# Probing only the even rows of a sorted segment mean, and fetching the odd rows' boundaries from their neighbours

## The chip, the cores and the metric

The kernel runs on one core of a Trainium2 chip. The time is the device time of one execution in microseconds (us). A run's time is about 2 us longer than the span of the instructions in its profile. A run is marked slow when it lies more than 1.5% above the fastest of the same kernel; ratios use fast runs alone.

Engines: DVE is VectorE, ACT is ScalarE, POOL is GpSimd, SP is SyncE, whose queue issues the large loads. PE (TensorE) does next to nothing here.

## The reference

```python
def setup_inputs():
    n = 10_000_000
    num_segments = 10000
    return {
        "data": np.random.randn(n).astype(np.float32),
        "segment_ids": np.sort(np.random.randint(0, num_segments, n)),
    }

def reference(data, segment_ids):
    num_segments = int(segment_ids.max()) + 1
    sums = np.zeros(num_segments, dtype=np.float32)
    counts = np.zeros(num_segments, dtype=np.float32)
    np.add.at(sums, segment_ids, data)
    np.add.at(counts, segment_ids, 1)
    return sums / np.maximum(counts, 1)
```

The ids are sorted and 64 bits wide, and a segment has about 1,000 elements. So one need not read all 80 MB of ids: it is enough to find where each segment ends.

## The kernel before

Each of 128 partitions holds 78,125 consecutive elements, cut into 90 rows of `L = 875` (the last one shorter). A row is shorter than nearly every segment, so it contains at most one boundary, or the kernel takes a slow general path. For every row the kernel works in five steps:

1. *Probe*: 5 single ids per row, one every `S = 175`, loaded by the SP queue as 8-byte pieces (15 loads of 6 rows each).
2. *Look* (DVE, six small instructions for a group of 6 rows): from the probes, find the block of 175 ids in which the id changes.
3. *Fetch* (POOL): an indirect DMA brings that block, 175 ids from each partition, into a ring of 18 windows.
4. *Window sum* (ACT) and *cut* (DVE): the sum of the window's ids gives the exact boundary `KK`.
5. *Split* (DVE, the large one): the row's data left of the boundary is summed. ACT sums the whole row (*total*); right is total minus left.

The distance in rows between asking for a window and needing it is written into the program: the look, with its fetches, of the group that begins at row g runs after the split of row g−9 (`X_LOOK = 9`), and its cut after the split of row g−1. That is 8 rows between ask and use.

```python
GROUPS = [6] * 15
X_PROBE, X_DATA, X_LOOK, RING, HALVES = 11, 26, 9, 18, 66
# ... cut: constants, general path ...
    dpool = ctx.enter_context(tc.tile_pool(name="dpool", bufs=18))      # 18 tiles of two rows
# ...
    def load_probes(g):
        a = 0 if g == 0 else K * bounds[g] + 1
        b = min(K * bounds[g + 1] + 1, NPR)
        nc.sync.dma_start(out=pr_flat[:, a:b], in_=ids_p[:, a * S : (b - 1) * S + 1 : S])
# ... cut: first_look, steps s1 to s5; s5 makes IDX, the block's address, and ends with ...
            gather(g)

    def gather(g):
        for r in range(bounds[g], bounds[g + 1]):
            nc.gpsimd.indirect_dma_start(
                out=GT[:, r % RING, :], out_offset=None, in_=ids2d[:],
                in_offset=bass.IndirectOffsetOnAxis(ap=IDX[:, r : r + 1], axis=0),
                bounds_check=N - W, oob_is_err=False,
            )

    def add_ids(r):
        nc.scalar.activation(
            out=junk_a[:, 0:W], in_=gt32[:, r % RING, 0 : 2 * W : 2], func=ACT.Copy,
            accum_out=GS[:, r : r + 1],
        )

    def second_look(a, b):                                              # the cut
        def s1():
            nc.vector.scalar_tensor_tensor(
                out=KK[:, a:b], in0=YY[:, a:b], scalar=float(S // K), in1=GS[:, a:b],
                op0=ALU.mult, op1=ALU.subtract,
            )
# ...
    def total(r):
        nc.scalar.activation(out=junk_a[:, 0:n], in_=d, func=ACT.Copy, accum_out=t)

    def split(r):
        nc.vector.scalar_tensor_tensor(
            out=junk_v[:, 0:n], in0=iota[:, 0:n], scalar=KK[:, r : r + 1], in1=d,
            op0=ALU.is_lt, op1=ALU.mult, accum_out=A[:, r : r + 1],
        )
# ... cut: combining partitions, output; then the schedule ...
    for a, b in zip(bounds[1:], bounds[2:]):
        if a < HALVES:
            put(a - 1, second_look(a, b))
# ...
    for g in range(HEAD, NG):
        if g < NG - 1:
            put(max(bounds[g] - X_LOOK, 0), first_look(g), 5)
# ... per row r: add_ids up to row r + 6, then
            total(r)
            split(r)
            for f in after[r]:
                f()
```

Of the kernel before, what the change touches and what calls it, by code (L numbers as in the profile page):

```python
# [9 lines left out]
FP32 = mybir.dt.float32  # L10
BF16 = mybir.dt.bfloat16
I32 = mybir.dt.int32
# [5 lines left out]
P = 128  # L18
D = 78125
# [10 lines left out]
GROUPS = [6] * 15  # L30
X_PROBE = 11
X_DATA = 26
X_LOOK = 9
RING = 18
HALVES = 66
# [82 lines left out]
def kernel(  # L118
# [9 lines left out]
    assert N == P * D and NSEG == 10000 and sum(GROUPS) == NR  # L128
# [14 lines left out]
    def x_sum(r):  # L143
        return 6 if r < HALVES else 5


    pr = cpool.tile([P, NR + 1, K], I64, name="pr")
    pr_flat = pr.rearrange("p r k -> p (r k)")
    pr32 = pr.bitcast(I32)
    snt = cpool.tile([P, 1], I64, name="snt")  # L150
    snt32 = snt.bitcast(I32)
    NPR = (D + S - 1) // S
    assert NPR == (NR - 1) * K + 2

    bounds = [0]
    for g in GROUPS:
        bounds.append(bounds[-1] + g)

    def load_probes(g):
        a = 0 if g == 0 else K * bounds[g] + 1  # L160
        b = min(K * bounds[g + 1] + 1, NPR)
        nc.sync.dma_start(out=pr_flat[:, a:b], in_=ids_p[:, a * S : (b - 1) * S + 1 : S])
# [17 lines left out]
    GT = gpool.tile([P, RING, W], I64, name="GT")  # L180
    gt32 = GT.bitcast(I32)

    def view(ap, dims):
# [3 lines left out]
        out=gt32[:, :, 0 : 2 * W : 2], in_=view(q5[:, 0, 0:1], [[0, RING], [0, W]]), func=ACT.Copy  # L187
    )

    wb_i = cpool.tile([P, NR], I32, name="wb_i")  # L190
    wb = cpool.tile([P, NR], FP32, name="wb")
    nc.gpsimd.iota(wb_i[:, 0 : NR - 1], pattern=[[L, NR - 1]], base=-S, channel_multiplier=D)
    nc.gpsimd.iota(wb_i[:, NR - 1 : NR], pattern=[[0, 1]], base=(NR - 1) * L - TAIL, channel_multiplier=D)
    nc.vector.tensor_copy(out=wb, in_=wb_i)
    i_i = cpool.tile([P, L], I32, name="i_i")
# [42 lines left out]
    VI = pr32[:, :, 0]  # L238
    SG = cpool.tile([P, NR], FP32, name="SG")
    ST = cpool.tile([P, NR], FP32, name="ST")  # L240
    YY = cpool.tile([P, NR], FP32, name="YY")
    IDX = cpool.tile([P, NR], I32, name="IDX")
    GS = cpool.tile([P, NR], FP32, name="GS")
# [12 lines left out]
    def first_look(g):  # L256

        a, b = bounds[g], bounds[g + 1]
        n = b - a
        far = fpool.tile([P, n], FP32, name="far", bufs=3)  # L260
        last = b == NR
        v = nc.vector

        def s1():
            if last:
                m = NR * K + 1 - NPR
                v.tensor_copy(
                    out=pr_flat.bitcast(I32)[:, 2 * NPR : 2 * (NPR + m)].rearrange("p (a b) -> p a b", b=2),
                    in_=view(snt32[:, 0:1], [[0, m], [1, 2]]),
                )  # L270
            v.tensor_reduce(out=SG[:, a:b], in_=pr32[:, a:b, 0 : 2 * K : 2], axis=AX.X, op=ALU.add)  # L271

        def s2():
            v.scalar_tensor_tensor(  # L274
                out=ST[:, a:b], in0=VI[:, a + 1 : b + 1], scalar=float(K), in1=SG[:, a:b],
                op0=ALU.mult, op1=ALU.subtract,
            )

        def s3():
            v.tensor_scalar(out=far, in0=ST[:, a:b], scalar1=0.0, scalar2=FAR, op0=ALU.is_equal, op1=ALU.mult)  # L280

        def s4():
            v.tensor_add(out=ST[:, a:b], in0=ST[:, a:b], in1=far)  # L283

        def s5():
            for c, d, w in [(a, b - 1, S), (b - 1, b, TAIL)] if last else [(a, b, S)]:
                v.scalar_tensor_tensor(  # L287
                    out=IDX[:, c:d], in0=ST[:, c:d], scalar=float(w), in1=wb[:, c:d], op0=ALU.mult, op1=ALU.add
                )
            v.scalar_tensor_tensor(  # L290
                out=YY[:, a:b], in0=ST[:, a:b], scalar=float(K + 1), in1=SG[:, a:b], op0=ALU.mult, op1=ALU.add
            )
            if last:
                v.tensor_scalar(
                    out=tl, in0=ST[:, NR - 1 : NR], scalar1=-1.0, scalar2=float(TAIL - S),
                    op0=ALU.add, op1=ALU.mult,
                )
            gather(g)

        return [s1, s2, s3, s4, s5]  # L300

    def gather(g):
        for r in range(bounds[g], bounds[g + 1]):
            nc.gpsimd.indirect_dma_start(  # L304
                out=GT[:, r % RING, :],
                out_offset=None,
                in_=ids2d[:],
                in_offset=bass.IndirectOffsetOnAxis(ap=IDX[:, r : r + 1], axis=0),
                bounds_check=N - W,
                oob_is_err=False,  # L310
            )

    def add_ids(r):
        nc.scalar.activation(  # L314
            out=junk_a[:, 0:W], in_=gt32[:, r % RING, 0 : 2 * W : 2], func=ACT.Copy,
            accum_out=GS[:, r : r + 1],
        )

    def second_look(a, b):
        def s1():  # L320
            nc.vector.scalar_tensor_tensor(  # L321
                out=KK[:, a:b], in0=YY[:, a:b], scalar=float(S // K), in1=GS[:, a:b],
                op0=ALU.mult, op1=ALU.subtract,
            )
            if b == NR:
                nc.vector.tensor_add(out=KK[:, NR - 1 : NR], in0=KK[:, NR - 1 : NR], in1=tl)

        return [s1]
# [54 lines left out]
    bad = cpool.tile([P, 2 * NX + 8], FP32, name="bad")  # L383
# [14 lines left out]
    def edges(a, b):  # L398
        nc.vector.tensor_sub(out=BT[:, a:b], in0=VI[:, a + 1 : b + 1], in1=VI[:, a:b])
# [6 lines left out]
    def extend():  # L406

        def s1():
            nc.vector.tensor_sub(out=B[:, 0:E], in0=T[:, 0:E], in1=A[:, 0:E])
            nc.vector.tensor_copy(out=V[:, 0 : E + 1], in_=VI[:, 0 : E + 1])  # L410
            edges(0, E)
# [41 lines left out]
    def keys(a, b):  # L453
        def s1():
            if a == 0:
                nc.vector.tensor_add(out=base1, in0=VI[:, 0:1], in1=pin)

        def s2():
            v = VI[:, a:b] if b <= NR else V[:, a:b]
            nc.vector.tensor_scalar(  # L460
                out=KEY[:, PAD + a : PAD + b], in0=v, scalar1=base1[:, 0:1], scalar2=None, op0=ALU.subtract
            )
            if b <= NR:
                edges(a, b)
            if a == 0:
                nc.vector.tensor_sub(out=delta, in0=sp, in1=base1)
# [55 lines left out]
    def check_columns():  # L522
# [3 lines left out]
                out=bad[:, NC + i : NC + i + 1], in0=sp, scalar=float(c), in1=VI[:, r : r + 1],  # L526
                op0=ALU.add, op1=o,
            )
            for i, c, r, o in ((5, C1, R1, ALU.is_gt), (6, C2, RM, ALU.is_gt), (7, CA, RM - 1, ALU.is_le))
        ]  # L530
# [151 lines left out]
    def pick(e, o, c0, n, a, b):  # L682
# [3 lines left out]
        def s1():  # L686
            c = min(b, NR)
            e.tensor_scalar(
                out=KL[:, a - R1 : c - R1], in0=VI[:, a:c], scalar1=sp[:, 0:1], scalar2=None, op0=ALU.subtract
# [77 lines left out]
    NG = len(GROUPS)  # L767
# [3 lines left out]
    HEAD = 3  # L771

# [7 lines left out]
    for g in range(HEAD):  # L780
        after[-1] += first_look(g)
    after[-1] += second_look(0, GROUPS[0])
    for a, b in zip(bounds[1:], bounds[2:]):
        if a < HALVES:
            put(a - 1, second_look(a, b))
        else:
            put(a - 1, second_look(a, a + 3))
            put(a + 2, second_look(a + 3, b))
    for g in range(HEAD, NG):
        if g < NG - 1:  # L790
            put(max(bounds[g] - X_LOOK, 0), first_look(g), 5)
# [28 lines left out]
    look = bounds[NG - 1] - X_LOOK - 2  # L820
# [6 lines left out]
    put(look, first_look(NG - 1), 99)  # L827
    put(look + 2, counts(R1, RM), 2)
    put(look, pick(nc.gpsimd, pb[:, :, RE - RM :], C2, NO - C2, RE, R2), 99)
    put(look + 1, edges_of(RE, NR))  # L830
    put(look + 4, single(0, NX, bad[:, NX:NC]) + verdict())
    put(look + 4, [
        lambda: v.tensor_scalar(out=nbl, in0=BT[:, NR - 2 : NR], scalar1=-1.0, scalar2=None, op0=ALU.mult)
    ])
    after[look + 7].append(lambda: verdict_reg.append(nc.values_load(badi[0:1, 0:1], min_val=0, max_val=1)))
# [11 lines left out]
    pnext = 0  # L847
    nt = 0
    gs = 0
    for r in range(-X_PROBE - X_DATA, NR):  # L850
        while pnext < NG and bounds[pnext] <= r + X_PROBE + pnext // (NG - 1) + X_DATA:
            load_probes(pnext)
            pnext += 1
            if pnext == 1:
                load_data(0)
                nt = 1
        while nt < NT and 2 * nt <= r + X_DATA:
            load_data(nt)
            nt += 1
# [5 lines left out]
        if r == -1:  # L865
            for f in after[r][: 5 * HEAD]:
                f()
        while r >= -1 and gs < NR and gs <= r + x_sum(gs):
            add_ids(gs)
            gs += 1  # L870
        if r == -1:
            for f in after[r][5 * HEAD :]:
                f()
        if r >= 0:
            total(r)
            split(r)
            for f in after[r]:
                f()
# [31 lines left out]
```

## Time and profile before

| | before |
|---|---|
| time, median of 3 (lowest to highest) | 189.97 us (189.69 to 190.56) |
| packets under 512 bytes | 60,016 |
| DMA share by stretch of time, from the windows view: 0–23, 23–60, 60–100, 100–140, 140–175, 175–190 us | 0.97, 1.07, 1.03, 1.03, 1.06, 0.12 |
| DVE busy / ACT busy / POOL busy | 140.9 / 136.5 / 99.8 us |
| last data packet ends | 177.4 us |
| row 24 / row 88 split begins | 63.4 / 183.8 us |

The profiled execution is marked slow (192.2 us).

The first lines are from the page of the kernel before: the busy tenths of DVE and DMA in 40 slices, the packets, and the share of 16 engines' time that each queue's packets took (q1 loads data and probes, q0 the fetches).

```profile
DVE  6521295969478792956978999566899969999991
...
DMA  6999999999999999999999999999999999999100
...
DMA packets 70163, 54.61 MB, mean 287 GB/s; under 512 B 60016, under 2 KB 60584, under 8 KB 70151
...
q1 hardware_dynamic: 64219, 40.50, 73.0%
q0 software_dynamic: 5760, 14.01, 23.2%
```

DMA is at nine tenths or more in 36 of 40 slices, DVE is not, and the traffic ends with the work.

The costliest groups on the same page: busy us, mean ns of one, then the idle time just before these instructions and what ended most of it.

```profile
L304 POOL DMA_INDIRECT GT<-in_segment_ids_dram,IDX x90 | 90.9, 1010 | 70.1 <-ACT junk_a L314 28.1
L339 DVE SCALAR_TENSOR_TENSOR junk_v<-iota,q,data_t 128x875 bf16<-128x875 f32 x90 | 100.4, 1116 | 7.4 <-DMA data_t<-in_data_dram 6.0
...
L314 ACT ACTIVATE junk_a<-GT 128x175 bf16<-128x175 int32 x90 | 32.4, 361 | 41.9 <-DMA GT<-in_segment_ids_dram,IDX 37.0
L321 DVE SCALAR_TENSOR_TENSOR q<-YY,GS 128x6 f32<-128x6 f32 (+1 forms) x19 | 3.2, 171 | 27.1 <-ACT junk_a L314 18.2
```

L304 is the fetch, L339 the split, L314 the window sum, L321 the cut. The waits view of the same kernel (us in total, times, longest):

```profile
ACT junk_a L314 <- DMA GT<-in_segment_ids_dram,IDX: 37.0, 22, 8.6
...
DVE q L321 <- ACT junk_a L314: 18.2, 8, 3.6
DVE q L321 <- issue: 7.6, 1, 7.6
DVE junk_v L339 <- DMA data_t<-in_data_dram: 6.0, 6, 1.9
```

How long a fetch takes is seen in the chain of waits (start us, us, what):

```profile
12.42 1.00 POOL GT L304
...
15.03 6.80 DMA GT<-in_segment_ids_dram,IDX
...
59.67 7.07 DMA GT<-in_segment_ids_dram,IDX
...
143.78 7.02 DMA GT<-in_segment_ids_dram,IDX
...
155.22 19.10 DMA data_t<-in_data_dram
```

A fetch takes about 7 us here from the start of its POOL record to landing, while that record lasts 1.0 us. The chain is made of fetches and of data by turns; the last long piece is 19.1 us of data. This agrees with the Trainium skill (Perfetto Trace Analysis, "DMA Instruction — SWDGE (GPSIMD)"), which says that the profiler's end of such an instruction is the end of descriptor generation and not of the data's movement.

### The profile page before, as it was taken

The page shows a single profiled execution, that of the slowest core. Times are in us where ns is not written, and L with a number is a line of the kernel's source. Part 1 is how long each engine was busy: PE and PEld are TensorE (multiplying, and loading weights), DVE is VectorE, ACT ScalarE, POOL GpSimd, SP SyncE. Part 2 cuts the span into 40 slices and gives each one's busy share as a digit, 9 for nine tenths or more (in the row PEclk, how much of TensorE's full clock was granted, in tenths as well). Part 3 has the DMA queues.
Part 4 walks back from the last instruction along what each step waited for, and adds up shares of the span by engine and source line. Part 5 has one row for each costly group of instructions (what it writes and reads, how often), then busy time and mean ns, then how long its engine had stood idle before and what let it go on. Part 6 is the DMA issues. An engine that isn't in the chain of part 4 may idle for free.

```text
span 190.2 us, 1434 instructions
## 1 busy us (share of the span) xinstructions
PE 1.6 (1%) x6; PEld 1.4 (1%) x6; DVE 140.9 (74%) x438; ACT 136.5 (72%) x362; POOL 99.8 (52%) x119
## 2 busy tenths in 40 slices
PE   0000000000002000000000000000000000010000
PEld 0000000000001000000000000000000000010000
DVE  6521295969478792956978999566899969999991
ACT  8011498995989499698685948959868594999930
POOL 5577875065753737266272572726638278782000
DMA  6999999999999999999999999999999999999100
GB/s 29 174 188 414 271 330 413 174 405 261 331 412 176 401 284 297 412 147 374 311 284 408 138 370 339 266 392 186 401 301 274 299 349 412 397 405 399 54 0 8
DMA packets 70163, 54.61 MB, mean 287 GB/s; under 512 B 60016, under 2 KB 60584, under 8 KB 70151
## 3 DMA queue, kind: packets, MB, share of 16 engines
q1 hardware_dynamic: 64219, 40.50, 73.0%
q0 software_dynamic: 5760, 14.01, 23.2%
q14 instruction: 12, 0.10, 0.2%
q10 hardware_dynamic: 172, 0.00, 0.1%
HBM read 56.59 MB, written 0.04 MB: 298 GB/s over the span
## 4 chain that ended last, share of the span: by engine, by line
DMA 45%; issue 27%; ACT 9%; POOL 8%; DVE 7%; POOLq 0%; ACTq 0%; DVEq 0%
DMA GT<-in_segment_ids_dram,IDX 23%; DMA data_t<-in_data_dram 22%; POOL GT L304 7%; ACT junk_a L334 5%; ACT junk_a L314 4%; DVE junk_v L339 2%; DVE jj L235 1%; POOL i_i L197 0%; POOLq L304 0%; DVE most L744 0%; DVE add L736 0%; DVE PS L561 0%; DVE add L744 0%; DVE ps L558 0%; DVE most L750 0%
## 5 line engine op out<-in xcount | busy, mean ns | idle before, releaser
L304 POOL DMA_INDIRECT GT<-in_segment_ids_dram,IDX x90 | 90.9, 1010 | 70.1 <-ACT junk_a L314 28.1
L339 DVE SCALAR_TENSOR_TENSOR junk_v<-iota,q,data_t 128x875 bf16<-128x875 f32 x90 | 100.4, 1116 | 7.4 <-DMA data_t<-in_data_dram 6.0
L334 ACT ACTIVATE junk_a<-data_t 128x875 bf16<-128x875 f32 x90 | 83.6, 929 | 3.5 <-ACT junk_a L314 0.7
L314 ACT ACTIVATE junk_a<-GT 128x175 bf16<-128x175 int32 x90 | 32.4, 361 | 41.9 <-DMA GT<-in_segment_ids_dram,IDX 37.0
L321 DVE SCALAR_TENSOR_TENSOR q<-YY,GS 128x6 f32<-128x6 f32 (+1 forms) x19 | 3.2, 171 | 27.1 <-ACT junk_a L314 18.2
L314 ACT ACTIVATION_READ_ACCUMULATOR junk_a<-GT 128x1 f32 x90 | 16.8, 186 | 0.0
L334 ACT ACTIVATION_READ_ACCUMULATOR junk_a<-data_t 128x1 f32 x90 | 16.8, 186 | 0.0
L339 DVE DVE_READ_ACCUMULATOR junk_v<-iota,q,data_t 128x1 f32 x90 | 7.4, 82 | 0.0
L271 DVE TENSOR_REDUCE SG<-pr 128x6 f32<-128x30 int32 x15 | 2.7, 180 | 5.4 <-DMA pr<-in_segment_ids_dram 5.3
L186 ACT ACTIVATE GT<-q 128x3150 int32<-128x3150 f32 x1 | 3.0, 2998 | 0.0
L280 DVE TENSOR_SCALAR far<-ST 128x6 f32<-128x6 f32 x15 | 2.6, 171 | 0.5
L287 DVE SCALAR_TENSOR_TENSOR IDX<-ST,wb 128x6 int32<-128x6 f32 (+2 forms) x16 | 2.6, 165 | 0.5
L274 DVE SCALAR_TENSOR_TENSOR ST<-pr,SG 128x6 f32<-128x6 int32 x15 | 2.5, 165 | 0.5
L283 DVE TENSOR_TENSOR ST<-ST,far 128x6 f32<-128x6 f32 x15 | 2.5, 165 | 0.5
L290 DVE SCALAR_TENSOR_TENSOR YY<-ST,SG 128x6 f32<-128x6 f32 x15 | 2.4, 158 | 0.0
L235 DVE CAST jj<-jj_i 128x128 f32<-128x128 int32 x1 | 1.5, 1484 | 0.7 <-POOL jj_i L234 0.7
L186 ACT ACT_TABLE_LOAD x1 | 1.3, 1283 | 0.7 <-PEq L894 0.7
L703 POOL TENSOR_SCALAR pb<-pb 128x168 f32<-128x168 f32 (+1 forms) x2 | 1.6, 784 | 0.2
L589 DVE TENSOR_TENSOR_SCAN FFP<-NBP,FFP,XX 128x16 f32<-128x16 f32 (+2 forms) x4 | 1.5, 382 | 0.0
L543 PE MATMUL badp<-bads,ones 128*128 128x1 f32 x2 | 0.6, 362 | 106.3 <-DVE bads L542 106.3
L583 DVE TENSOR_TENSOR q<-T,q 128x44 f32<-128x44 f32 (+3 forms) x4 | 0.7, 180 | 0.9 <-DVE RB L574 0.4
L736 POOL TENSOR_TENSOR xa<-pa,RG 128x528 f32<-128x528 f32 x1 | 1.2, 1247 | 0.2 <-DVE RG L733 0.2
(129 smaller groups left out, 44.3 us busy)
## 6 DMA issues: line engine op xcount, KB each, us to landing
data_t<-in_data_dram SPq DMA_DIRECT2D x44, 875.0 KB
GT<-in_segment_ids_dram,IDX POOLq DMA_INDIRECT x90
data_t<-in_data_dram SPq DMA_DIRECT2D x1, 437.5 KB
pr<-in_segment_ids_dram SPq DMA_DIRECT2D x13, 30.0 KB
data_t<-in_data_dram SPq DMA_DIRECT2D x1, 125.0 KB
out_dram<-OUT SPq DMA_DIRECT2D x1, 36.6 KB
pr<-in_segment_ids_dram SPq DMA_DIRECT2D x1, 31.0 KB
pr<-in_segment_ids_dram SPq DMA_DIRECT2D x1, 26.0 KB
```

The lines of the kernel that those rows point to most:

```text
L186: nc.scalar.activation(out=gt32[:, :, 0 : 2 * W : 2], in_=view(q5[:, 0, 0:1], [[0, RING], [0, W]]), func=ACT.Copy)
L235: nc.vector.tensor_copy(out=jj, in_=jj_i)
L271: v.tensor_reduce(out=SG[:, a:b], in_=pr32[:, a:b, 0 : 2 * K : 2], axis=AX.X, op=ALU.add)
L274: v.scalar_tensor_tensor(out=ST[:, a:b], in0=VI[:, a + 1 : b + 1], scalar=float(K), in1=SG[:, a:b], op0=ALU.mult, op1=ALU.subtract,)
L280: v.tensor_scalar(out=far, in0=ST[:, a:b], scalar1=0.0, scalar2=FAR, op0=ALU.is_equal, op1=ALU.mult)
L283: v.tensor_add(out=ST[:, a:b], in0=ST[:, a:b], in1=far)
L287: v.scalar_tensor_tensor(out=IDX[:, c:d], in0=ST[:, c:d], scalar=float(w), in1=wb[:, c:d], op0=ALU.mult, op1=ALU.add)
L304: nc.gpsimd.indirect_dma_start(out=GT[:, r % RING, :], out_offset=None, in_=ids2d[:], in_offset=bass.IndirectOffsetOnAxis(ap=IDX[:, r : r ...
L314: nc.scalar.activation(out=junk_a[:, 0:W], in_=gt32[:, r % RING, 0 : 2 * W : 2], func=ACT.Copy, accum_out=GS[:, r : r + 1],)
L321: nc.vector.scalar_tensor_tensor(out=KK[:, a:b], in0=YY[:, a:b], scalar=float(S // K), in1=GS[:, a:b], op0=ALU.mult, op1=ALU.subtract,)
L334: nc.scalar.activation(out=junk_a[:, 0:n], in_=d, func=ACT.Copy, accum_out=t)
L339: nc.vector.scalar_tensor_tensor(out=junk_v[:, 0:n], in0=iota[:, 0:n], scalar=KK[:, r : r + 1], in1=d, op0=ALU.is_lt, op1=ALU.mult, accum_ ...
```

## The change

The intent is to save DMA time. Neighbouring boundaries lie about one segment apart, so an odd row's boundary must lie near the middle between the boundaries of the even rows around it. So only even rows are probed (6 points each, so that the row's last id is known too). An odd row's 208 ids are fetched around the mean of its neighbours' exact boundaries. A check at the end finds any boundary that lay outside its 208 ids and then takes the general path. The last 7 rows are all probed, and the row totals on ACT run up to 6 rows ahead in the first part.

```diff
-GROUPS = [6] * 15
+EVEN = [3, 3, 3, 3, 6, 6, 6, 6, 6]          # groups of even rows
+WO = 208
+    def load_pairs(a, b):                    # 42 loads of one even row each
+        nc.sync.dma_start(
+            out=pr[:, a:b, :],
+            in_=bass.AP(ids_p.tensor, ids_p.offset + 2 * L * a, [list(ids_p.ap[0]), [2 * L, b - a], [S, K + 1]]),
+        )
# ... cut: gather and add_ids now take both kinds, in the order in which they were asked ...
+    def even_cut(a, b):
+        def s1():
+            add_ids(asked[False, b - 1] + 1)
+            nc.vector.scalar_tensor_tensor(
+                out=rows_of(a, b), in0=YY[:, a:b], scalar=float(S // K), in1=GS[:, a:b],
+                op0=ALU.mult, op1=ALU.subtract,
+            )
+    def between(c, d):
+        def s1():
+            nc.vector.tensor_add(out=SM[:, c:d], in0=rows_of(c, d), in1=rows_of(c + 1, d + 1))
+        def s2():
+            nc.vector.scalar_tensor_tensor(
+                out=IDXO[:, c:d], in0=SM[:, c:d], scalar=0.5, in1=FB[:, c:d], op0=ALU.mult, op1=ALU.add
+            )
+    def odd_cut(c, d):
+        def s1():
+            add_ids(asked[True, d - 1] + 1)
+            nc.vector.tensor_sub(out=KK[:, 2 * c + 1 : 2 * d : 2], in0=YO[:, c:d], in1=GSO[:, c:d])
+    def chain(k):
+        c, d = odds(k)
+        e, b = even_cut(bounds[k], bounds[k + 1]), between(c, d)
+        return e + b[:2] + [lambda: gather(True, c, d)] + b[2:]
# ... cut: the first groups have places of their own in the schedule; the later ones: ...
+        if k >= 6:
+            put(b - 24, ask(k, 0, 3))
+            put(b - 19, ask(k, 3, 6))
+        if k >= 5:
+            put(b - 9, chain(k), 3)
+        put(b - 2, odd_cut(c, c + 3))
+        put(b + (1 if k == NG - 1 else 3), odd_cut(c + 3, d))
# ...
+    def ahead(r):
+        return max(0, 6 - max(r, 0) // 8)
```

So an odd window needs an even window first: even fetch, ACT sum, even cut, middle, odd fetch, ACT sum, odd cut.

## The prediction

> **What bounds the kernel now.** The DMA engines. The page's 40 slices show DMA at 9 tenths or more from the second slice to the 37th. The table of stretches gives a DMA share of 0.97 to 1.07 up to 175 us and 0.12 after it, while DVE is busy 141 of 190 us and ACT 137. The chain of waits is 45% DMA. Data rows land 2 to 10 us before they are used. The last data packet ends at 177 us; the DVE tail after it takes 9 us, the output write 4.
>
> By packet records, the time of all packets over 16 engines: data 104 us (7,000-byte packets, 292 ns mean), window fetches 43 us (90 of 128 x 1,400 bytes; 208 ns per 4,200 bytes), probes 34 us (57,216 packets of 8 bytes, 9.5 ns each): 183 us in about 175, so a few per cent overlap. The Trainium skill (DMA: Bandwidth & Descriptors, "Rules for kernel authors") says that a strided last dimension lowers to one descriptor per element; the 57,216 packets agree.
>
> **What the change removes.** Probes fall from 447 per partition to 42 x 6 + 37 = 289: 20,224 packets fewer, at 9.5 ns over 16 engines 12.0 us. Stretches with probes have up to 18.8 packets in flight against 16.3 elsewhere, so part of a probe's time is hidden; I count 8 to 12 us.
>
> **What it adds.**
> - 41 of the 90 fetches grow from 1,400 to 1,664 bytes. Cost goes by bytes (49 ns per KB in packets of 2,800 and 4,200): 41 x 0.48 us x 0.19 = 3.7 us. POOL stays at 91 us for 90 fetches.
> - DVE: 411 instructions against 348, the new ones of 0.15 to 0.18 us: about 10 us, to 151 us, off the DMA path but some 90% between 23 and 170 us.
> - A dependent chain: even fetch, ACT sum, even cut, middle, odd fetch, ACT sum, odd cut. A fetch took about 7 us in the chain of waits. Even fetches are asked about 24 rows early, odd ones 9 (some 16 us), and POOL needs 1.3 us for each: tight, but it fits.
> - ACT: larger sums, 41 x 0.05 = 2 us.
>
> **On the critical path.** The stream shortens by 8 to 12 less 3.7, that is 4.5 to 8 us, and the end of data moves to about 170 us. The first rows start at about the same time (22.6 us), since only three even rows head the chain. The tail stays. I give back 1 us for DVE waits on odd windows.
>
> The window arithmetic, redone on the host for this draw, puts no odd boundary outside its 208 ids, so the slow general path is not taken.
>
> **Predicted time:** 184.3 us, range 180.5 to 189; faster by over 2% (below 186.2 us) 0.70, within 2% 0.25, slower by over 2% 0.05.
>
> **What would show each step.** Packets under 512 B near 40,000 instead of 60,016. The hardware queue's packet time lower by about 12 us, the software queue's higher by 3 to 4. Last data packet near 170 us. DMA at 9 tenths in all slices up to there. DVE busy near 151 us, ACT near 139. DVE's waits for ACT's window sums below about 20 us in total.
>
> **What would make it wrong.** If probes mostly hide behind data packets, the gain is under 3 us: "same". If the odd chain stalls DVE (waits well over 20 us, DMA slices below 9 because tiles come free late), the gain is lost or worse. If probes cost their full 12 us or more, because they hold up the fetches queued with them, the time nears 180 us.

## More of the kernel before

The experiments ran on several chips, so runs of different sets are compared by their ratios to the kernel before, which ran beside each of them. The kernel after was timed in its own set only.

## The result, and the profile after

| | before | after |
|---|---|---|
| time, median | 189.90 us (4 runs) | 202.44 us (201.5 to 203.42, 4 runs) |
| ratio of fast runs | | 1.0655, 95% interval 1.0594 to 1.0715 |
| packets under 512 bytes | 60,016 | 39,632 |
| last data packet ends | 177.4 us | 160.6 us |
| DMA share, the stretches of before's table | 0.97, 1.07, 1.03, 1.03, 1.06, 0.12 | 0.95, 1.09, 1.06, 1.04, 0.71, 0.01 |
| DVE busy 23–60 / 60–100 / 100–140 us | 28.5 / 29.5 / 32.4 | 22.5 / 25.3 / 34.9 |

A ratio is the mean time of one kernel's fast runs over the mean of the other's fast runs of the same rounds, so it is not quite the ratio of the medians quoted. The result is correct and no boundary missed its window.

The page of the kernel after, the same lines:

```profile
DVE  6415387931865832979396999994689999949991
...
DMA  5999999999999999999999999999999954000000
...
DMA packets 49781, 55.67 MB, mean 279 GB/s; under 512 B 39632, under 2 KB 40200, under 8 KB 49767
...
q1 hardware_dynamic: 43835, 40.33, 62.2%
q0 software_dynamic: 5760, 15.22, 23.4%
```

The saving took place. Shares times span: q1's packets took 0.730 × 190.2 = 138.8 us before and 0.622 × 199.7 = 124.2 us after; q0's 44.1 and 46.7 us. DMA is at nine tenths or more up to the 32nd slice, and the data is in 17 us earlier than before. But DVE has hollows in the first half (slices of 3, 1 and 2 tenths), and at the data's end it still has some 20 of the 90 rows to split.

The groups of the kernel after (L450 the split, L342 the fetch, even and odd, L437 the odd cut, L368 the even cut):

```profile
L450 DVE SCALAR_TENSOR_TENSOR junk_v<-iota,q,data_t 128x875 bf16<-128x875 f32 x90 | 100.3, 1115 | 0.3
...
L342 POOL DMA_INDIRECT GT<-in_segment_ids_dram,IDXO x41 | 41.3, 1007 | 54.5 <-ACT junk_a L445 39.1
...
L437 DVE TENSOR_TENSOR q<-YO,GSO 128x3 f32<-128x3 f32 (+1 forms) x14 | 2.3, 162 | 27.6 <-ACT junk_a L356 13.0
...
L368 DVE SCALAR_TENSOR_TENSOR q<-YY,GS 128x6 f32<-128x6 f32 (+1 forms) x9 | 1.5, 164 | 10.2 <-ACT junk_a L356 9.5
```

POOL stood 54.5 us before its odd fetches. The split has only 0.3 us of idle time before it: data is always there. Nearly all of the waiting is at the cuts, 27.6 + 10.2 us, in place of 27.1 + 7.4 us at cut and split. The waits view (L356 is the window sum on ACT):

```profile
ACT junk_a L356 <- DMA GT<-in_segment_ids_dram,IDXO: 28.2, 16, 5.9
...
DVE q L437 <- ACT junk_a L356: 13.0, 4, 4.7
DVE q L437 <- issue: 10.6, 3, 7.0
DVE q L368 <- ACT junk_a L356: 9.5, 6, 4.9
```

These totals are hardly larger than before's. Where the time went is seen when the splits are lined up by row (start of the split, and the landing of the row's last data packet, both taken from the trace's records). The data packets carry no row; they are counted off in the order of their starts, 128 to a tile of two rows, and as the packets of neighbouring tiles overlap, these landings can be early by up to some 3 us. Those of row 88 are exact, as its packets have a size of their own (counted off, they came out 0.8 and 2.7 us too early):

| row | data landed before | split before | data landed after | split after | split after − before |
|---|---|---|---|---|---|
| 0 | 7.6 | 22.6 | 6.8 | 19.8 | −2.8 |
| 12 | 34.5 | 41.7 | 36.2 | 51.9 | +10.2 |
| 24 | 57.5 | 63.4 | 59.3 | 80.3 | +16.9 |
| 48 | 107.2 | 110.1 | 100.1 | 123.3 | +13.2 |
| 72 | 155.4 | 155.9 | 138.2 | 164.4 | +8.5 |
| 88 | 177.0 | 183.8 | 159.8 | 193.2 | +9.4 |

The first 24 rows lose 17 us. Rows 24 to 88 then take 112.9 us instead of 120.4 (119.1 in the fast run e3, where row 24 begins at 64.7): the saving does appear there, and it is less than the loss. In the kernel after, the data of row 12 lies ready about 16 us before it is used, that of row 48 about 23 us and that of row 88 33 us. Of the 27.6 us at the odd cuts 20.1 us fall between rows 0 and 24, where the schedule leaves an odd window 1, 4, 7, 5 and 3 rows from ask to cut (groups 0 to 4).

One stall, step by step. The timeline of POOL in the kernel after (start us, us, instruction, [idle before and what ended it]):

```profile
35.58 1.00 POOL L342 DMA_INDIRECT GT<-in_segment_ids_dram,IDX  x1 [0.30 <-DVE FE L311]
...
38.19 1.00 POOL L342 DMA_INDIRECT GT<-in_segment_ids_dram,IDX  x1 [0.31 <-issue]
...
42.11 1.00 POOL L342 DMA_INDIRECT GT<-in_segment_ids_dram,IDX  x1 [0.31 <-issue]
52.62 1.00 POOL L342 DMA_INDIRECT GT<-in_segment_ids_dram,IDXO  x1 [9.51 <-ACT junk_a L445]
53.92 1.00 POOL L342 DMA_INDIRECT GT<-in_segment_ids_dram,IDXO  x1 [0.30 <-issue]
55.23 1.00 POOL L342 DMA_INDIRECT GT<-in_segment_ids_dram,IDXO  x1 [0.31 <-issue]
```

The timeline of ACT in the same time:

```profile
48.59 0.94 ACT L445 ACTIVATE junk_a<-data_t 128x875 bf16<-128x875 f32 x1 [2.45 <-DMA data_t<-in_data_dram]
...
50.61 0.36 ACT L356 ACTIVATE junk_a<-GT 128x175 bf16<-128x175 int32 x1
...
59.39 0.38 ACT L356 ACTIVATE junk_a<-GT 128x208 bf16<-128x208 int32 x1 [2.58 <-DMA GT<-in_segment_ids_dram,IDXO]
...
61.84 0.39 ACT L356 ACTIVATE junk_a<-GT 128x208 bf16<-128x208 int32 x1 [0.87 <-DMA GT<-in_segment_ids_dram,IDXO]
```

And that of DVE:

```profile
46.17 0.17 DVE L437 TENSOR_TENSOR q<-YO,GSO 128x3 f32<-128x3 f32 x1 [4.72 <-ACT junk_a L356]
49.20 0.17 DVE L295 CAST VV<-pr 128x12 f32<-128x12 int32 x1 [2.86 <-DMA pr<-in_segment_ids_dram]
...
51.09 0.16 DVE L368 SCALAR_TENSOR_TENSOR q<-YY,GS 128x3 f32<-128x3 f32 x1 [0.60 <-ACT junk_a L356]
...
51.69 0.16 DVE L419 SCALAR_TENSOR_TENSOR IDXO<-SM,FB 128x3 int32<-128x3 f32 x1
...
57.82 0.21 DVE L325 SCALAR_TENSOR_TENSOR YY<-ST,SG 128x6 f32<-128x6 f32 x1
62.35 0.16 DVE L437 TENSOR_TENSOR q<-YO,GSO 128x3 f32<-128x3 f32 x1 [4.32 <-ACT junk_a L356]
```

POOL is idle for 9.51 us, and for nearly all of it the odd addresses don't exist yet. ACT sums the windows in the order of their fetches: the three even windows of this group, asked from 35.58 to 38.19, are summed by 50.61, after ACT had stood until 48.59 for the data of a row total (those at 42.11 and just before it belong to the next group). DVE comes to their cut late as well: it had stood 4.72 us at the odd cut before, and then 2.86 us for probes (49.20). The cut runs at 51.09, and the addresses are there at 51.85 (51.69 + 0.16). The profile puts the end of POOL's idle time, 0.8 us later, down to ACT. Then three odd fetches go out, the last at 55.23, and its ids are summed at 61.84, 5.6 us after its record on POOL ended. DVE ran the five rows in between in 6.2 us, was ready for the odd cut at 58.03 (57.82 + 0.21), and stands 4.32 us. From the odd addresses to the odd cut, 51.85 to 62.35, it is 10.5 us; from the group's first even fetch, 35.58, it is 27 us.

The probes that DVE waited for until 49.20 are those of rows 36 to 46. Their look stands in the schedule after row 10, though the first fetches that need it are asked after row 17 only. DVE took them in the order of its program, so the next split waited for something that it did not need.

### The profile page after: what moved, and what is told of

It is laid out like the page before. It is cut to its first block, busy times and chain, and to the rows that moved or that the text cites. A ratio compares the mean times of both kernels' runs of the same rounds, so it can differ in the third digit from the quotient of the medians.

```text
span 199.7 us, 1544 instructions
## 1 busy us (share of the span) xinstructions
PE 1.6 (1%) x6; PEld 1.4 (1%) x6; DVE 143.1 (72%) x501; ACT 138.2 (69%) x362; POOL 99.7 (50%) x121
## 2 busy tenths in 40 slices
DMA packets 49781, 55.67 MB, mean 279 GB/s; under 512 B 39632, under 2 KB 40200, under 8 KB 49767
## 4 chain that ended last, share of the span: by engine, by line
issue 28%; DMA 24%; SPq 19%; DVE 15%; ACT 9%; POOL 3%; POOLq 0%; ACTq 0%; DVEq 0%
SPq L163 14%; DMA GT<-in_segment_ids_dram,IDXO 10%; DMA data_t<-in_data_dram 10%; DVE junk_v L450 8%; SPq L178 6%; ACT junk_a L356 4%; ACT junk_a L445 4%; DMA GT<-in_segment_ids_dram,IDX 4%; POOL GT L342 3%; DVE sel L781 0%; DVE sel L772 0%; DVE most L869 0%; DVE PS L686 0%; DVE FFP L714 0%; DVE add L861 0%
## 5 line engine op out<-in xcount | busy, mean ns | idle before, releaser
L450 DVE SCALAR_TENSOR_TENSOR junk_v<-iota,q,data_t 128x875 bf16<-128x875 f32 x90 | 100.3, 1115 | 0.3
L445 ACT ACTIVATE junk_a<-data_t 128x875 bf16<-128x875 f32 x90 | 83.6, 929 | 17.7 <-DMA data_t<-in_data_dram 14.3
L342 POOL DMA_INDIRECT GT<-in_segment_ids_dram,IDXO x41 | 41.3, 1007 | 54.5 <-ACT junk_a L445 39.1
L342 POOL DMA_INDIRECT GT<-in_segment_ids_dram,IDX x49 | 49.3, 1005 | 17.8 <-issue 12.4
L356 ACT ACTIVATE junk_a<-GT 128x175 bf16<-128x175 int32 (+1 forms) x90 | 33.5, 372 | 33.2 <-DMA GT<-in_segment_ids_dram,IDXO 28.2
L437 DVE TENSOR_TENSOR q<-YO,GSO 128x3 f32<-128x3 f32 (+1 forms) x14 | 2.3, 162 | 27.6 <-ACT junk_a L356 13.0
L356 ACT ACTIVATION_READ_ACCUMULATOR junk_a<-GT 128x1 f32 x90 | 16.8, 187 | 0.0
L368 DVE SCALAR_TENSOR_TENSOR q<-YY,GS 128x6 f32<-128x6 f32 (+1 forms) x9 | 1.5, 164 | 10.2 <-ACT junk_a L356 9.5
L450 DVE DVE_READ_ACCUMULATOR junk_v<-iota,q,data_t 128x1 f32 x90 | 7.4, 83 | 0.0
L295 DVE CAST VV<-pr 128x12 f32<-128x12 int32 (+1 forms) x9 | 1.7, 185 | 6.1 <-DMA pr<-in_segment_ids_dram 6.1
L194 ACT ACTIVATE GT<-q 128x3744 int32<-128x3744 f32 x1 | 3.5, 3527 | 0.0
L311 DVE TENSOR_SCALAR FE<-ST 128x6 f32<-128x6 f32 (+2 forms) x10 | 1.9, 191 | 0.2
L325 DVE SCALAR_TENSOR_TENSOR YY<-ST,SG 128x6 f32<-128x6 f32 (+2 forms) x10 | 1.7, 170 | 0.0
L316 DVE TENSOR_TENSOR ST<-ST,FE 128x6 f32<-128x6 f32 (+2 forms) x10 | 1.6, 160 | 0.1
```

The costliest lines, as they stand in the source:

```text
L194: nc.scalar.activation(out=gt32[:, :, 0 : 2 * WO : 2], in_=view(q5[:, 0, 0:1], [[0, RING], [0, WO]]), func=ACT.Copy)
L295: v.tensor_copy(out=VV[:, 2 * a : 2 * b].rearrange("p (a b) -> p a b", b=2), in_=pr32[:, a:b, 0 : 2 * K + 1 : 2 * K],)
L311: v.tensor_scalar(out=FE[:, a:b], in0=ST[:, a:b], scalar1=0.0, scalar2=FAR, op0=ALU.is_equal, op1=ALU.mult)
L325: v.scalar_tensor_tensor(out=YY[:, a:b], in0=ST[:, a:b], scalar=float(K + 1), in1=SG[:, a:b], op0=ALU.mult, op1=ALU.add)
L342: nc.gpsimd.indirect_dma_start(out=GT[:, len(asked) % RING, 0:n], out_offset=None, in_=ids2d[:], in_offset=bass.IndirectOffsetOnAxis(ap=id ...
L356: nc.scalar.activation(out=junk_a[:, 0:n], in_=gt32[:, i % RING, 0 : 2 * n : 2], func=ACT.Copy, accum_out=to[:, r : r + 1],)
```

## The experiments

Fifteen kernels ran, each with 4 runs. The expectations quoted name their theories themselves. Some compute a wrong result; there the final verdict that would choose the general path is forced to zero, so that the same instructions run. "Before" is always the kernel before on the same chip in the same rounds.

The first theory (A) was that in the kernel after ACT stands behind totals whose data has not landed, so that the window sums come late. The rival (B) was that the fetch loop itself, from ask to cut, is too long for the distance it is given. A third question was whether the DMA stream was a bound at all.

### e1: the row totals no longer run ahead (kernel after)

```diff
     def ahead(r):
-        return max(0, 6 - max(r, 0) // 8)
+        return 0
```

> The kernel after, with ACT's row totals recorded at their own row instead of up to six rows ahead. Theory A (ACT stands in its queue behind totals whose data has not landed, 14.3 us in the kernel after, and the window sums behind them come late, so odd cuts and DVE come late): the waits of ACT for data fall under 3 us, DVE's waits for window sums fall by 5 to 10 us, time 193 to 198 us. Rival B (the fetch chain even fetch, even cut, odd fetch, odd cut is itself too long for the rows at the head): the same 202 us within 2 us, because the sums were waiting for their fetch anyway.

Measured: 202.88 us against 190.63, ratio 1.0632 [1.0567, 1.0697]; correct. That is no gain on 1.0655. ACT's totals wait 0.5 us for data instead of 14.3, and the waits came back as waits for windows, 28.1 us for odd and 13.5 us for even ones. So Theory A's forecast falls. But the test is masked in the head. DVE's 4.72 us at the odd cut are gone (it ran at 41.68), and the next instruction waits longer for the probes of rows 36 to 46:

```profile
50.22 0.17 DVE L295 CAST VV<-pr 128x12 f32<-128x12 int32 x1 [8.38 <-DMA pr<-in_segment_ids_dram]
```

This wait ended at 48.7 to 50.2 us in all five kernels with this head (after, e1, e9, e11, e18), so none of them reached row 12 before 50 us. No run has this look at a later row.

### e2 and e6: the kernel before, with a third of its probes not loaded

```diff
+UNLOADED = (3, 5, 7, 9, 11)
     def load_probes(g):
-        a = 0 if g == 0 else K * bounds[g] + 1
+        if g in UNLOADED:
+            return
+        a = K * bounds[g]                                                          # e2
+        a = 0 if g == 0 else K * bounds[g] + (0 if g - 1 in UNLOADED else 1)       # e6
# the looks of these groups read the probes of the group before; verdict forced to 0
```

> The kernel before, with the probes of 5 of its 15 groups not loaded (their looks use the group in front; result wrong on purpose, the verdict forced to the fast path). Some 18,600 of 57,216 small packets go, nearly what the change removes, and nothing else changes. If the first step of the prediction holds (the stream bounds the kernel before and probes cost 8 to 12 us of it): 179 to 183 us. If probes hide behind other packets: 187 us or more.

> The run with fewer probes again, without a fault of that edit (two probe loads overlapped by one column, so they waited for one another at the head and the first row began 4 us late). Theory D (the kernel before is bound twice: the stream and the row loop of ACT and DVE with the fetches in front of it are nearly equally long, so taking probes away alone buys little): 186 to 189 us, with the data again landed near 160 us. Prediction's first step (the stream alone bounds): 179 to 183 us.

Their outputs are wrong, which doesn't matter for the times. In e2 neighbouring probe loads overlapped by one id, which made them wait for one another, and the first split started 4 us late; so e2 (192.0 against 190.63, 1.0061 [0.9989, 1.0133]) tells little. e6 has no overlap: 188.23 against 189.58 us, ratio 0.9929 [0.9875, 0.9982]. There are 41,379 packets under 512 bytes instead of 60,016, and the data ends at 161.6 us. A stream shorter by 16 us at its end gave 0.7%. The waits view of e6 says why:

```profile
ACT junk_a L318 <- DMA GT<-in_segment_ids_dram,IDX: 35.7, 16, 7.7
DVE q L325 <- ACT junk_a L318: 29.0, 10, 7.6
```

The splits have no wait for data any more in that view; what is left on DVE's side is mostly waits for windows, 29.0 us of them. So the DMA stream was not the only bound of the kernel before: without a third of the probes, something else, by these waits the fetch loop, holds the time within 1% of where it was.

### e3 and e18: 63 small DVE instructions more, in the kernel before and after

```diff
             split(r)
+            if r < 63:                       # e18: r >= 27
+                nc.vector.tensor_scalar(out=spare, in0=rp[:, 0:6], scalar1=1.0, scalar2=None, op0=ALU.add)
```

> The kernel before, with 63 more small DVE instructions (128 x 6), one after each of the first 63 rows: the number that the change adds. Rival C (the added DVE work itself makes the kernel after slow): 6 to 10 us slower, 196 to 200 us. Theory A and rival B: DVE has slack while the DMA stream bounds, so 190 to 192 us.

> The kernel after with 63 more small DVE instructions, one after each row from 27 on. In the kernel before 63 of them cost 0.15%, within noise. If DVE is full in the later rows of the kernel after: 206 to 210 us. If it has slack there: 202 to 204 us.

e3: 191.22 against 190.63, 1.0015 [0.9954, 1.0076]. e18: 200.86 against 190.21, 1.0552 [1.0497, 1.0608], with DVE busy at 148.2 us instead of 143.1. So 63 small DVE instructions cost nothing that can be seen, in either kernel (in the kernel after, the rows before 27 were left alone). That e18 comes out at 1.0552, with more work than the kernel after and its 1.0655, also shows how well ratios of different sets compare: to about 1%, or 2 us.

### e7, e8, e9: half of the row totals left out

```diff
-        nc.scalar.activation(out=junk_a[:, 0:n], in_=d, func=ACT.Copy, accum_out=t)
+        if r % 2 == 0:
+            nc.scalar.activation(out=junk_a[:, 0:n], in_=d, func=ACT.Copy, accum_out=t)
# T set to 0 first; e7: kernel before, e8: kernel before with e6's edit, e9: kernel after
```

> The kernel before without ACT's row total in every second row (result wrong on purpose): about 45 us less work in ACT's queue, the stream unchanged. Theory D: the stream then bounds alone, so 185 to 189 us. If ACT alone bounds: under 180 us.

> Both edits in one: fewer probes and half of the row totals. Theory D: clearly more than the sum of the two single gains, 172 to 180 us. If DVE or the fetch latency bounds and neither ACT nor the stream: no better than the better of the two.

> The kernel after without ACT's row total in every second row (result wrong on purpose). If the in-order ACT queue with its 180 sums bounds the kernel after: 185 us or less. Rival B (the fetch chain at the head and DVE's fuller queue): at most 5 us gained, 197 to 202 us.

Their outputs are wrong, which doesn't matter for the times. e7: 188.73 against 189.58, 0.9972 [0.9909, 1.0034]. e8: 184.69, 0.9736 [0.9684, 0.9789]. e9: 196.39, 1.0368 [1.029, 1.0447]. Taking some 45 us of work from ACT (91 us busy left in e7) is worth nothing alone. With fewer probes it is worth 2%, less than I expected, and in the kernel after about 5.5 us (1.0655 − 1.0368 of 190), or 3.5 us against e18's ratio. In e8 ACT then stood 66.5 us for fetches and DVE still 27.5 us for window sums. ACT's load is one part of the loop; with half of the totals gone, fetches still hold it.

### e11: the odd windows asked around a constant middle (kernel after)

```diff
         def s1():
-            nc.vector.tensor_add(out=SM[:, c:d], in0=rows_of(c, d), in1=rows_of(c + 1, d + 1))
+            nc.vector.tensor_add(out=SM[:, c:d], in0=MC[:, c:d], in1=MC[:, c:d])
# chain(k): the middle and the odd fetch now come before the even cut
```

> The kernel after, with the odd windows fetched around a constant middle instead of the mean of the two exact even boundaries (result wrong on purpose, the verdict forced to the fast path). Every instruction, fetch and probe stays; only the wait of the odd fetch for the even sums and the even cut goes, and it is asked before the even cut. Theory B (two fetches in a row before an odd row can be split cost the time, above all in rows 0 to 24, which the kernel after reaches 17 us later than the kernel before): the 24th row begins 6 to 17 us earlier and the time is 188 to 197 us. Rival (something else at the head, such as probes or data landing late): 200 us or more.

This takes away the wait of the odd fetch for the even sums and the even cut, and leaves all transfers and the rows at which they are asked. Its output is wrong, which doesn't matter for the time. 194.46 against 189.89, ratio 1.0229 [1.0133, 1.0326]. Against the kernel after's 1.0655 that is 0.0426 × 190 = 8 us of the 12.5 us that the change lost, against e18's 1.0552 it is 6 us. But row 24 still began only at 77.2 us (80.3 in the kernel after), and DVE still stood 25.9 us at the odd cuts, 20.5 of them before row 24. So the serial wait is a part, and in the head the few rows from ask to cut, and the probes that land late (e1), are still there.

### e12 and e15: the first 24 rows probed as before, even rows only from there on

```diff
+H = 24
+HEAD = [3, 3, 6, 6, 6]
-EVEN = [3, 3, 3, 3, 6, 6, 6, 6, 6]
+EVEN = [6] * 5
# with looks, fetches and cuts of their own for rows 0 to 23, placed in the schedule by hand
```

> The kernel after with rows 0 to 23 all probed as the kernel before probes them, in groups of 3, 3, 6, 6 and 6, and the even-only scheme from row 24 on with its old schedule. Right result. Theory B with the split of the account (the head lost 17 us, rows 24 to 88 took 7 us less than before): the 24th row begins at 60 to 66 us and the time is 182 to 189 us, so it beats both kernels. If the loss is spread over all rows or sits in the later ones: 195 us or more.

> Probed head again, mended: in the first try ACT stood behind row totals whose data came late (its first window sum at 24 us against 14 us in the kernel before). Now totals stay at their own row, the even probes of the later groups come after the head's, and the odd windows are asked 12 rows ahead instead of 9. Right result. Theory B: the 24th row begins at 63 to 68 us and the time is 183 to 190 us. If later rows cost the time: 194 us or more.

e12 is correct: 199.45 against 189.89, 1.0501 [1.0426, 1.0575], row 24 at 79.1 us. The expectation failed, and the waits view points to my own schedule: totals ran ahead before the first window sums, and DVE stood once for 16.6 us. e15 put this right, with totals not ahead: 197.54 against 191.13, 1.0444 [1.0338, 1.0551], row 24 at 72.5 us. Its result is wrong by a slip of mine (the cut of rows 12 to 17 stands one row too late), which leaves the amount of work as it is. Its data in the head landed late, between 44 and 58 us for rows 12 to 20; I put this down to the even rows' probes, which were loaded far ahead, but no run tests it. Both are half-misses: probing the head as before is not enough by itself.

### e13 and e14: the kernel before, with windows asked 4 rows earlier

```diff
-X_PROBE = 11
+X_PROBE = 15
-X_LOOK = 9
+X_LOOK = 13
# e14: with e6's missing probes too
```

> The kernel before with each group's look and fetches placed 13 rows ahead instead of 9, and the probe loads 4 rows earlier; right result, the same work. Theory D with fetch latency as its third bound (ask, fetch, sum and cut of six windows take longer than the 8 rows that cover them; DVE waits 20 us for window sums between 22 and 81 us): those waits halve, but the stream still takes its time, so 186 to 190 us.

> The same earlier asks in the kernel with fewer probes (result wrong on purpose). If fetch latency is what kept the saved probes from paying (the first such kernel gained 0.7%): 179 to 184 us, more than the two single edits together. If it is only ACT's queue: 186 us or more.

e13 is correct: median 190.91 against 191.13, ratio of fast runs 1.0112 [0.9995, 1.023] (three of the seven runs before were slow ones and left out), a little above what was expected. e14 is wrong as e6 is: 178.42 us, ratio 0.9466 [0.9335, 0.9596]. The verdict on record is "unclear" for both (as for e11 and e15), and the runs of the kernel before lay in two groups on this chip, near 189 and near 191.5 us; but e14's slowest run, 180.83 us, lies 4% below the fastest of before, 188.56 us. The waits views of e13 and of e14:

```profile
DVE junk_v L339 <- DMA data_t<-in_data_dram: 20.5, 13, 3.1
...
DVE q L321 <- ACT junk_a L314: 11.4, 2, 6.4
```

```profile
DVE q L325 <- issue: 16.4, 4, 11.7
...
DVE q L325 <- ACT junk_a L318: 2.7, 3, 1.0
```

In e13 the waits at the cuts fall from 27.1 to 13.7 us, and waits for data come in their place, 20.5 instead of 6.0 us: the time stays. In e14 no wait of the splits for data is left in the view; of the 20.3 us at the cuts 11.7 us are one wait, before the first row, and the splits of rows 24 to 88 take 103 us instead of 120. The four cells together:

| ratio to before | asked 8 rows ahead | asked 12 rows ahead |
|---|---|---|
| all probes | 1 | 1.011 (e13) |
| a third of the probes gone | 0.993 (e6) | 0.947 (e14) |

This is the experiment that decides. The kernel before has two bounds of nearly the same height, the DMA stream and the fetch loop. To lower one of them gives 0.7% or nothing; to lower both gives 5.3%. (e13 and e14 also load the probes 4 rows earlier; this was not tried apart.)

### e16 and e17: the change, with room in the fetch loop

```diff
-RING = 18
+RING = 24
-dpool bufs=18
+dpool bufs=16
+H = 24                                       # e17: 48; rows below H probed as before, 13 rows ahead
-            put(b - 24, ask(k, 0, 3))
-            put(b - 19, ask(k, 3, 6))
-            put(b - 9, chain(k), 3)
+        put(max(b - 24, 3), ask(k, 0, 6), 99)
+        put(b - 12, chain(k), 3)
# each window sum placed some 6 rows before its use; totals not ahead
```

> Rows 0 to 23 all probed with a lead of 13 rows, the even-only scheme from row 24 with even windows asked 24 rows ahead and odd ones 11 to 12, every window sum placed at a row of its own about six rows ahead of its use; window ring of 24 instead of 18, 16 data tiles instead of 18 to make room. Right result. If the lead is what the kernel after lacks: 181 to 188 us. If the DVE work in later rows is what remains: 190 to 196 us with the 24th row at 62 to 67 us, as in the kernel before, and DVE without waits after it.

> The same with the even-only scheme from row 48 only: 17 odd rows instead of 29 go unprobed, so 60% of the saving, with fewer added DVE instructions. Right result. Lead theory: 182 to 187 us. DVE theory: better than e16 by 2 to 4 us.

e16 is correct and beats both kernels: 187.84 against 190.21 us, ratio 0.9864 [0.9824, 0.9904]. That is 15 us less than the kernel after (0.0791 × 190) and 13 us less than e18 of the same set, though under the 2% that I would call faster. Row 24 begins at 68.6 us and row 88 at 179.7. Its waits view:

```profile
DVE junk_v L505 <- DMA data_t<-in_data_dram: 15.2, 9, 2.6
...
DVE q L384 <- ACT junk_a L411: 10.4, 4, 3.9
...
DVE q L492 <- ACT junk_a L411: 3.8, 2, 3.2
```

L505 is the split, L384 the cut of the probed rows, L492 the odd cut. The odd cut stands 3.8 us for its 29 odd rows, in place of 27.6 us for 41, and the largest wait is now for data, 15.2 us. e17 keeps the full probes up to row 48: 191.64, ratio 1.0081 [1.0017, 1.0145], where I expected a gain. It has 51,808 packets under 512 bytes and stands 20.5 us for data. No experiment settles whether the head's probes or the two data tiles fewer cost it that.

## Why the prediction was wrong

*The stream.* The prediction put the packets under 512 bytes near 40,000 (39,632), q1's packet time 12 us lower (14.6) and q0's 3 to 4 us higher (2.6), and the end of the data near 170 us (160.6). What it cites from the Trainium skill (DMA: Bandwidth & Descriptors, "Rules for kernel authors"), one descriptor for each element of a strided last dimension, holds here: 57,216 packets of 8 bytes for 447 probes of 128 partitions. This half of the mechanism was right, and larger than predicted.

*The load on the engines.* DVE busy was predicted at 151 us and was 143.1, ACT at 139 and was 138.2. By e3 and e18 such a load is free from row 27 on, and in the kernel before. The general path was not taken, as predicted.

*The step that failed* is the one "on the critical path": "The stream shortens by 8 to 12 less 3.7 … and the end of data moves to about 170 us", from which the time was taken, with "1 us for DVE waits on odd windows" given back. It supposes that the time follows the end of the data. It did not: the data ended 17 us earlier and the time grew by 12.5 us, while DVE stood 27.6 us at the odd cuts. In the kernel before this was half of the truth: e6 shortens the stream alone and the time moves 0.7%; e14 shortens the stream and the loop, and it moves 5.3%. The lines for it were on the page of before: 27.1 us of idle time before the cuts, against 7.4 before the splits. The prediction itself says that data rows "land 2 to 10 us before they are used", so DVE was not waiting for them. It named "below about 20 us" as what DVE's waits for window sums would be, without seeing that the cuts stood 27 us already; after the change it was 37.8 us. A DMA share near 1 in all slices says that the engines had something to move, not that nothing else would have held the kernel up. The Trainium skill (Perfetto Trace Analysis, "Identifying the Most-Contended Engine") has a warning for such a share: for DMA it says to take HBM utilization in place of occupancy, since 16 engines make occupancy misleading. The profile before has 298 GB/s over the span, by an estimate 83% of the 358 GB/s that the same page ("Engine Utilization") gives as a core's share when both cores of a pair read; a core alone, it says, can pull more, and the best slices here moved 414. But neither number proves a bound or its absence; e6 and e14 do.

*The term that was mis-sized* is "odd ones 9 (some 16 us) … tight, but it fits". In the steady part the odd fetch goes out after the split of row b−8 and the first odd cut comes after that of row b−2: 6 rows, not 9, and in the head 1 to 7. Measured in the trace of the kernel after, from the odd addresses to the end of the third odd sum it took 9.9 to 11.1 us in the last four groups, and 10.5 us in the stall shown. DVE ran the six rows in that time in 7.1, 7.7, 10.9 and 10.9 us, and stood 4.0, 3.0, 0 and 0 us; in the head it ran five rows in 6.2 us and stood 4.3, and three rows in 4.0 us and stood 7.0. So there was little slack or none, and any faster pace, which was the aim, makes DVE wait. The kernel before was already in this state: in its groups that begin at rows 18 to 60, the loop from the split after which a group is asked (look, six fetches, six sums) took 16.3 to 17.7 us, the eight rows, with the one cut between them, 13.1 to 16.9 us, and DVE stood at seven of the eight cuts (16.2 to 16.9 and 12.5 to 19.1 us in the fast run e3, also seven of eight). ACT is part of that loop: it went over to the sixth sum with no more than 0.03 us of idle time, so by then the sums stood behind row totals and not only behind fetches, which fits the 2% of e8. e13 with 12 rows and e16 with 9 for the odd windows show shorter waits with more distance, though e16 changed other things too.

*"I give back 1 us for DVE waits on odd windows."* Without the wait for the even cut the kernel after wins back 6 to 8 us (e11). The largest loss is in the head, by the table of rows, and there the record shows two causes side by side: odd windows asked 1 to 7 rows ahead (20.1 us at their cuts), and a look at row 10 that stops DVE until probes land at 49 us (e1). e16, which changes the lead, the head's probes, the ring, the place of the sums and the totals together, wins back 13 to 15 us.

*What the prediction named as its danger* was right in kind: "If the odd chain stalls DVE (waits well over 20 us …), the gain is lost or worse". The stated chance of 0.05 for slower was too small, as the loop above was to be had from the trace of before.

*What stays open.* How the head's loss divides between its few rows from ask to cut, the loading of probes and the order of the sums on ACT: e1 moves the totals alone and meets the probes, e11 takes the even wait alone, no run moves the look at row 10 or the rows from ask to cut alone, and e12 and e15 changed several at once and met new waits. The chain of waits of the kernel after puts 19% of its span on the SP queue, 14% on the small probe loads, all before 41 us; whether fewer, larger loads would help the head is untried, since a kernel that merged them would not build (the access pattern has one dimension too many). And it is open why e16 stays 4% above e14. It loads 45,792 small packets to e14's 41,377, has fewer data tiles, and its odd fetches stand behind six even ones on POOL (at 71.8 us odd addresses are there, the first odd fetch goes out at 77.1), but no run separates these.

## What to carry to other kernels

A fully busy DMA does not prove that DMA alone sets the time: take some of its load away, even with a wrong result, and see whether the time follows, before building a change that saves it. If an edit gives nothing, try it together with an edit of the other suspect, since two bounds of equal height hide each other (0.7% and nothing alone, 5.3% together). When a saving is bought with one more dependent fetch, count the loop in time, fetch issue plus landing plus sum, and give it more rows from ask to use than it needs at the pace hoped for, the first rows included. And place no instruction in an engine's program earlier than its result is needed if its input may land late: here DVE stood 1.9 to 8.4 us for probes that it needed only later.

## What the Trainium skill lacked or had wrong

- DMA: Bandwidth & Descriptors, "Anatomy of one DMA — SWDGE (gpsimd) path", fits a transfer as 2.0 us plus its bytes over 436 GB/s. For a fetch of 128 × 1,400 bytes that would be, as an estimate, 2.4 us. In this kernel, beside a full stream of data and probes, such a fetch took about 7 us in the chain of waits (6.8 to 7.1 in the lines shown). The page has no figure for an indirect fetch under load; the prediction had to take it from the trace.
- The same page, "Rules for kernel authors", says that a strided last dimension costs one descriptor per element, but not what such a descriptor costs, and the page has no measured time for packets of 8 bytes. Here 57,216 of them took 9.5 ns each on one of the 16 engines (34 us of all 16).
- Perfetto Trace Analysis, "Identifying the Most-Contended Engine", tells to optimize the most-contended engine first. It has nothing on two bounds of the same height at the same time, as here (ratios 0.993 and 1.011 alone, 0.947 together), nor on testing a supposed bound by taking its load away.
- No page says how to find the distance that is needed between asking for a window and using it. Here 8 rows (13.1 to 16.9 us) were less than the loop of 6 fetches mostly took (16.3 to 17.7 us), and 12 rows halved the waits at the cuts (27.1 to 13.7 us).
